# A decoder layer in one fp32 kernel: memory laid out from two ends, loads of the next phase begun early, x1 kept transposed, and GpSimd making sums and down's blocks

## The chip, the cores and the metric

The kernel runs on one core of one Trainium2 chip. It has five engines that each take their instructions in order: PE (TensorE, matrix products), DVE (VectorE), ACT (ScalarE), POOL (GpSimd) and SP (SyncE), which here issues every data transfer. An engine that has to wait stands, and everything behind the waiting instruction stands with it. The metric is the device time of one execution in microseconds (us); less is better.

## The reference

Inputs are x (1, 2048, 1024), a conditioning vector and the weights, all fp32. One layer has two sub-layers, each followed by a layer norm:

```python
for l in range(DEPTH):                                   # DEPTH = 1
    mod = (sc @ w_ada[l] + b_ada[l])[:, None, :]
    sh1, s1, g1, sh2, s2, g2 = jnp.split(mod, 6, axis=-1)
    u = x * (1 + s1) + sh1
    x = layer_norm(DN_ALPHA * x + g1 * token_mixer(u, ...), ln1_g[l], ln1_b[l])
    u = x * (1 + s2) + sh2
    x = layer_norm(DN_ALPHA * x + g2 * swiglu(u, w_gate[l], w_up[l], w_down[l]), ln2_g[l], ln2_b[l])

def swiglu(u, w_gate, w_up, w_down):                     # 1024 -> 2816 -> 1024
    return (jax.nn.silu(u @ w_gate) * (u @ w_up)) @ w_down
```

token_mixer holds two kinds of windowed attention, whose outputs are lifted to 1024 channels (w_a, w_b), merged by sigmoid gates and projected by w_o. The x after the first layer norm is called x1 below.

## The kernel before

Every product is made with fp32 accuracy from parts: ScalarE rounds an operand to its high part (hi, L114), VectorE subtracts this from the operand (lo, L115), and PE makes three passes, hi x hi, hi x lo and lo x hi. This pair of instructions is a split.

**Attention, to about 830 us**, is left as it is by the change. **The mixer's end, 830 to 1500 us**, goes over four chunks of 512 tokens in the order 3, 0, 1, 2. For each, PE makes the gates (L147, mm<-ut,whl), w_a and w_b, then the out-projection with w_o (L881, outputs in banks s and o). VectorE adds the residual and takes statistics (L887 to L890) and finishes the layer norm (layer_norm, L737 and L738, on tiles named xr), and SP stores x1 to DRAM (x_s). The next chunk's gates do not read this.

**The FFN, 1500 to 2430 us**, multiplies by w_gate and w_up with a Strassen-Winograd scheme of seven products. It runs in 44 sets: two passes p over halves of the tokens, 11 groups g of 256 of the 2816 columns, and gate and up in turn. A set is 84 matmuls of 128x512: seven products of 12, in the order 1, 6, 2, 7, 5, 4, 3. Set 0 of each pass and the last set of each pass run by block (k = 0 to 3, all seven products for each k), the others by product. A set needs left factors, made once per pass by left(p, k) from x1, and right factors, made for each set by the class Right:

- left loads four blocks of x1, PE transposes them (L945), ScalarE applies scale and shift (L946), VectorE makes four sums (left_sums, L907 to L910), and two splits give the tiles cb.
- Right loads 1 MB of weights (L959, tile g, "the raw block"), VectorE makes four sums (right_sums, L913 to L916, t1 to t4), and splits give the units a, b, c and d (tiles w). The raw block of set N+1 is asked for while set N runs.
- Of the results, ScalarE and VectorE form the four output quarters (L996, silu L1007, up times gate L1019). Product 3 adds into the bank that product 5 left, so VectorE has to have read the bank by then. After each up set GpSimd makes four left sums of h (L907 to L910), and h and the sums are stored in DRAM (h_s).

**The down phase, 2430 us to the end**, uses the same seven products over 77 steps of 24 matmuls (L1149, acc<-hw). For each step factors(m, g) loads 128x1024 of h_s and 128x512 of w_down or of its sums (t_s), and splits it (tile hw). right_of makes the sums of w_down on VectorE during the first 11 steps. first_half, second_half and evict multiply by g2 (g2b, on GpSimd at L1168 or VectorE), add the residual and make the last layer norm.

Each phase's buffers lie in pools that are opened when the phase begins and closed at its end; a pool's buffer is reused only when everything that reads it has ended. The order of the instructions on each engine is settled when the kernel is built, in the order of the code with a scheduler's shifts.

## Time and profile before

| | |
|---|---|
| median of 3 runs | 2906.16 us (2901.02 to 2907.05) |
| the profiled execution | 2909.35 us, its span 2907.5 us |
| mean granted clock of TensorE | 0.975 |
| TensorE busy | 2762.3 us, 95% |
| VectorE busy | 1959.4 us, 67% |
| ScalarE busy | 1161.7 us, 40% |
| GpSimd busy | 255.8 us, 9% |

The span runs from the first to the last instruction. The granted clock is the share of TensorE's full clock that the chip gave in that stretch, 1.00 being all of it. Busy time leaves out waits, so what an engine lacks to the span is time in which it stood. In the rows below, "out<-in" names the tiles that an instruction writes and reads.

### The profile page before, as it was taken

To read this page: it belongs to the slowest core of one execution; us is meant where nothing else is said; L and a number is where in the kernel's file an instruction comes from. 1 tells how busy PE (TensorE), PEld (TensorE's weight loads), DVE (VectorE), ACT (ScalarE), POOL (GpSimd) and SP (SyncE) were. 2 spreads that over 40 slices of the span, in tenths; PEclk is the share of its full clock that TensorE was granted. 3 is DMA by queue.
4 is the path that set the end of the run, shared out by engine and by line. 5 is a ranking of instruction groups with operands and counts; after the bars stand their busy time and mean duration, and the time that the engine had idled before them with its cause. 6 is when DMAs were issued, how large, how long until landed. Compare 5 with 4: busy or idle time off the path is not lost. (4 is left out here: it accounts for less than half of the span.)

```text
span 2907.5 us, 37081 instructions
## 1 busy us (share of the span) xinstructions
PE 2762.3 (95%) x13715; PEld 2292.2 (79%) x13715; DVE 1959.4 (67%) x3459; ACT 1161.7 (40%) x1918; POOL 255.8 (9%) x163
## 2 busy tenths in 40 slices
PE   7999999999999999999978999996999997999986
PEld 6888888887887788888866888885888886888875
DVE  7656567778768876756367666667666664543499
ACT  3555455666695443342324223234222222333220
POOL 0000000000000000000000111111111110000233
PEclk9999999999999999999989999997999998999998
DMA  9764646776788664744323223333233225984463
GB/s 281 198 157 127 164 117 145 165 176 141 158 204 287 198 207 144 219 127 150 110 95 98 94 94 98 109 123 98 95 109 109 94 95 209 329 279 143 144 218 125
DMA packets 569797, 452.98 MB, mean 156 GB/s; under 512 B 205640, under 2 KB 486288, under 8 KB 569616
## 3 DMA queue, kind: packets, MB, share of 16 engines
q1 hardware_dynamic: 569616, 450.62, 53.0%
q8 instruction: 107, 1.75, 0.3%
q14 instruction: 74, 0.61, 0.1%
HBM read 322.80 MB, written 91.82 MB: 143 GB/s over the span
## 5 line engine op out<-in xcount | busy, mean ns | idle before, releaser
L992 PE MATMUL mm<-cb,w 128*128 128x512 f32 x3696 | 860.2, 394 | 31.7 <-ACT w L114 12.3
L992 PEld LDWEIGHTS mm<-cb,w 128*128 128x128 f32 x3696 | 698.7, 190 | 184.9 <-ACT w L114 13.6
L147 PE MATMUL mm<-ut,whl 128*128 128x512 f32 x3072 | 727.7, 394 | 3.9 <-DVE ut L115 3.5
L147 PEld LDWEIGHTS mm<-ut,whl 128*128 128x128 f32 x3072 | 571.8, 188 | 131.3 <-DVE ut L115 7.0
L1149 PE MATMUL acc<-hw 128*128 128x512 f32 x1848 | 427.5, 394 | 36.8 <-ACT hw L114 18.7
L1149 PEld LDWEIGHTS acc<-hw 128*128 128x128 f32 x1848 | 351.4, 191 | 112.9 <-ACT hw L114 19.2
L115 DVE TENSOR_TENSOR whl<-raw,whl 128x1024 fp32r<-128x1024 f32 (+1 forms) x228 | 265.6, 1165 | 154.2 <-ACT whl L114 149.1
L114 ACT ACTIVATE whl<-raw 128x1024 fp32r<-128x1024 f32 (+1 forms) x228 | 230.3, 1010 | 308.6 <-PE mm L147 71.6
L114 ACT ACTIVATE w<-g 128x1024 fp32r<-128x1024 f32 (+1 forms) x176 | 167.0, 952 | 367.6 <-PE mm L992 329.1
L115 DVE TENSOR_TENSOR hw<-raw,hw 128x1536 fp32r<-128x1536 f32 x77 | 147.8, 1919 | 121.9 <-ACT hw L114 118.1
L114 ACT ACTIVATE hw<-raw 128x1536 fp32r<-128x1536 f32 x77 | 114.7, 1490 | 284.6 <-PE acc L1149 119.2
L115 DVE TENSOR_TENSOR w<-g,w 128x1024 fp32r<-128x1024 f32 (+1 forms) x176 | 194.4, 1108 | 37.5 <-ACT w L114 37.3
L560 PE MATMUL mm<-whl,ut 128*128 128x256 f32 (+1 forms) x1152 | 209.8, 340 | 0.0
L560 PEld LDWEIGHTS mm<-whl,ut 128*128 128x128 f32 x1152 | 202.7, 236 | 2.4
L996 DVE TENSOR_TENSOR t<-mm,t 128x512 f32<-128x512 f32 x138 | 94.9, 688 | 134.7 <-PE mm L992 134.7
L287 DVE TENSOR_TENSOR ehl<-te,ehl 128x512 f16<-128x512 f32 (+1 forms) x160 | 98.1, 615 | 109.9 <-ACT ehl L286 109.6
L147 PE MATMUL mm<-q,whl 128*128 128x512 f32 x576 | 138.2, 395 | 2.0 <-DVE q L115 1.2
L147 PEld LDWEIGHTS mm<-q,whl 128*128 128x128 f32 x576 | 109.9, 191 | 26.0 <-issue 1.5
L745 POOL TENSOR_TENSOR rs<-rs,mhalf 128x1 f32<-128x1 f32 x32 | 46.5, 1459 | 848.7 <-DVE rs L744 848.7
L907 POOL TENSOR_TENSOR g<-g 128x512 f32<-128x512 f32 x22 | 45.6, 2073 | 767.4 <-DVE g L1019 712.0
L276 DVE CUSTOM_DVE_ANT_0 te<-s,tab 128x256 f32<-128x256 f32 (+1 forms) x320 | 109.3, 382 | 1.7 <-PE s L264 1.4
L299 PE MATMUL o<-v,pt 128*128 128x192 bf16 x1096 | 92.3, 236 | 4.2 <-DMA pt<-ehl 4.2
(176 smaller groups left out, 2864.4 us busy)
## 6 DMA issues: line engine op xcount, KB each, us to landing
raw<-in_w_in_dram SPq DMA_DIRECT2D x132, 512.0 KB, 4.1
raw<-h_s SPq DMA_DIRECT2D x77, 512.0 KB, 3.7
g<-in_w_gate_dram SPq DMA_DIRECT2D x22, 1024.0 KB, 7.6
g<-in_w_up_dram SPq DMA_DIRECT2D x22, 1024.0 KB, 5.3
h_s<-g SPq DMA_DIRECT2D x22, 1024.0 KB, 5.1
h_s<-g SPq DMA_DIRECT2D x22, 768.0 KB, 3.5
raw<-in_w_ada_dram SPq DMA_DIRECT2D x32, 512.0 KB, 4.5
raw<-in_w_o_dram SPq DMA_DIRECT2D x32, 512.0 KB, 3.7
```

What stands on the lines that cost most here:

```text
L114: nc.scalar.activation(hi, src, AF.Copy)
L115: nc.vector.tensor_tensor(lo, src, hi.bitcast(F32), op=OP.subtract)
L147: nc.tensor.matmul(ps, lhs(k, a), rhs(k, b), start=i == 0, stop=i == n - 1)
L276: nc.vector.tensor_tensor_reduce(out=te[:, h, :nk], in0=ps[h], in1=tables[h][:, 256 - nk:], scale=1.0, scalar=-3e38, op0=OP.add, op1=OP.ma ...
L287: nc.vector.tensor_tensor(eh[:, 1], te[:, :, :nk], eh[:, 0], op=OP.subtract)
L299: nc.tensor.matmul(pv[:, h, a:], pt[:, (a * 2 + h) * nb + j], v[:, :3 - a], start=j == 0 and a == 0, stop=j == nb - 1 and a == 1)
L560: nc.tensor.matmul(ps[t][:, :n], lhs_of(us[k][a], t), whl[:, b, kk * n:(kk + 1) * n], start=k == 0 and i == 0, stop=k == KT - 1 and i == 2)
L745: nc.gpsimd.tensor_tensor(rs, rs, mhalf, op=OP.pow)
L907: eng.tensor_tensor(s[:, 0], a21, a22, op=OP.add)
L992: nc.tensor.matmul(ps, r.of(m, k, a), us[k][b][:, LEFT[m]], start=first and k == 0 and i == 0, stop=last and k == 3 and i == 2, skip_group ...
L996: nc.vector.tensor_tensor(out, ps, other, op=op)
L1149: nc.tensor.matmul(ps, hw[:, a, t * 128:(t + 1) * 128], hw[:, b, 1024:], start=first and i == 0, stop=last and i == 2, skip_group_check=True)
```

## The change

- Pools can be opened at either end of the memory (side="right"), so that buffers of the next phase are there while the current phase still holds its own. open_right opens the FFN's first buffers before the last out-projection of the mixer; open_down opens the down phase's before the last set of the FFN ends.
- x1 is also kept transposed in DRAM (xT_s). Chunks 3, 0 and 1 are transposed by PE at the chunk's end and copied by ScalarE; the 512 tokens of chunk 2 by turn, in sets 4 and 8 of the FFN. left_load then loads transposed blocks, without PE.
- GpSimd makes the left sums of the FFN's inputs (before: VectorE).
- down_right, after sets 2, 6, ..., 42: GpSimd scales w_down by g2 and makes its sums, eight blocks of a group go to t_s. The down phase reads them, and its multiplications by g2b are gone.
- All raw blocks, left blocks and down_right's two tiles share one pool of four buffers (g1). Before, six buffers g4 served these and h; now g4 has two, for h and its sums.
- The first half's layer norm in the down phase is done in two parts (first_left, first_right), its last part on ScalarE and GpSimd.

```diff
+    def g1():
+        return gp.tile([128, 4, 512], F32, name="g1")
...
+    def left_load(p, k):
+
+        e, s = g1(), g1()
+        nc.sync.dma_start(e[:, 1:3], dr(xT_s, (k + 4) * 128 * S + p * 1024, [[S, 128], [512, 2], [1, 512]]))
+        for hf in range(2):
+            nc.sync.dma_start(e[:, 3 * hf], dr(xT_s, k * 128 * S + p * 1024 + hf * 512, [[S, 128], [1, 512]]))
+        for kk, i in ((k, slice(0, 1)), (k, slice(3, 4)), (k + 4, slice(1, 3))):
+            nc.scalar.activation(e[:, i], e[:, i], AF.Identity, scale=mod[:, S2, kk:kk + 1],
+                                 bias=mod[:, SH2, kk:kk + 1])
+        left_sums(s, e[:, 0], e[:, 1], e[:, 3], e[:, 2], nc.gpsimd)
+        return e, s
+
+    def left_split(es, comb):
+
+        hi, lo = (comb.tile([128, 7, 512], F32R, name="cb") for _ in range(2))
+        split(hi[:, :3], lo[:, :3], es[0][:, :3])
+        split(hi[:, 3:], lo[:, 3:], es[1])
+        return hi, lo
+
+    def open_right():
+
+        nonlocal gp, comb, us01, es2, raw0, t0
+        gp = tile_pool(tc, "g1", 4, ctx, "right")
+        comb = tile_pool(tc, "comb1", 4, near, "right")
+        us01 = [left_split(left_load(0, k), comb) for k in range(2)]
+        raw0, t0 = load_right(w_gate, 0), g1()
+        gate_sums(t0, raw0)
+        es2 = left_load(0, 2)
...
+    def open_down():
+
+        nonlocal rawp, hwa, ready
+        rawp = tile_pool(tc, "raw5", 3, ctx, "right")
+        hwa = tile_pool(tc, "hwa", 3, ctx, "right")
+        ready = [factors(n) for n in range(AHEAD)]
...
+            if after is None:
+                outer.close()
+                open_right()
...
+            for k in range(KT if after is not None else 0):
+                ps = bank()
+                for b in range(4):
+                    nc.tensor.transpose(ps[:, b * 128:(b + 1) * 128], xr[b][:, k * 128:(k + 1) * 128], ident)
+                ub = ubp.tile([128, 512], F32, name="ub")
+                nc.scalar.activation(ub, ps, AF.Copy)
+                nc.sync.dma_start(xT_s[k, :, ch * 512:(ch + 1) * 512], ub)
...
+        g4 = pool("g4", 2, ph)
...
+        def down_right(g):
+
+            b, t = g1(), g1()
+            v = b.rearrange("p a n -> p (a n)").rearrange("p (f n) -> p f n", f=2)
+            nc.sync.dma_start(v, dr(w_down, 2 * g * 128 * D, [[D, 128], [128 * D, 2], [1, D]]))
+            for f in range(2):
+                nc.gpsimd.tensor_tensor(v[:, f], v[:, f], g2b, op=OP.mult)
+            right_sums(t[:, 0], t[:, 1], t[:, 2], t[:, 3], b[:, 0], b[:, 1], b[:, 2], b[:, 3], nc.gpsimd)
+            for i, x in enumerate((t, b)):
+                nc.sync.dma_start(dr(t_s, (g * 8 + i * 4) * 128 * 512, [[512, 128], [128 * 512, 4], [1, 512]]), x)
+
+        def turn(k0):
+
+            x, t = g1(), g1()
+            nc.sync.dma_start(x, dr(x1_s, 1024 * D + k0 * 128, [[D, 128], [128 * D, 4], [1, 512]]))
+            for k in range(4):
+                ps = mm_bank()
+                for b in range(4):
+                    nc.tensor.transpose(ps[:, b * 128:(b + 1) * 128], x[:, b, k * 128:(k + 1) * 128], ident)
+                nc.scalar.activation(t[:, k], ps, AF.Copy)
+            nc.sync.dma_start(dr(xT_s, k0 * 128 * S + 1024, [[S, 128], [128 * S, 4], [1, 512]]), t)
...
-            left_sums(s, e[:, 0], e[:, 1], e[:, 3], e[:, 2], nc.vector)
...
+        us = us01 + [left_split(es2, comb2), left_split(left_load(0, 3), comb2)]
         nxt = []
+
+        def between(k):
+            if k == 1:
+                near.close()
+                open_down()
...
+                             lambda k: nxt.append(left_split(left_load(1, k), comb if k < 2 else comb2)))
...
+            if n % 4 == 2:
+                down_right(n // 4)
+            if n in (4, 8):
+                turn(n - 4)
...
-            eng.tensor_tensor(y[:, hs], y[:, hs], g2b[:, hs], op=OP.mult)
...
-                w = xrp.tile([128, D], F32, name="xr")[:, :512]
-                nc.vector.tensor_tensor(w, ps, g2b[:, L], op=OP.mult)
-                nc.vector.tensor_tensor(x, x, w, op=OP.subtract)
-                nc.vector.bn_stats(sts[t][:, 0], x)
-                mv, rs = layer_norm(tmp, y, sts[t], l2g, l2b, t == 7)
+                nc.vector.tensor_tensor(x, x, ps, op=OP.subtract)
+                nc.vector.bn_stats(sts[t, 1][:, 0], x)
...
+        def first_left(t):
+            residual(y1[t], L, t, 0)
+            statistics(t, 0)
+            nc.vector.bn_stats(sts[t, 0][:, 0], y1[t][:, L])
+
+        def first_right(t):
             y = y1[t]
-            residual(y, slice(0, D), t, 0, nc.gpsimd)
-            st = tmp.tile([128, 2, 6], F32, name="st", bufs=9)
-            for n, hs in enumerate((L, R)):
-                nc.vector.bn_stats(st[:, n], y[:, hs])
-            layer_norm(tmp, y, st, l2g, l2b)
+            residual(y, R, t, 0)
+            nc.vector.bn_stats(sts[t, 0][:, 1], y[:, R])
+            mv, rs = layer_norm(tmp, y, sts[t, 0], l2g, l2b, True)
+            nm = tmp.tile([128, 1], F32, name="nm")
+            nc.vector.scalar_tensor_tensor(nm, mv[:, :1], -1.0, rs, op0=OP.mult, op1=OP.mult)
+            nc.scalar.activation(y, y, AF.Identity, scale=rs, bias=nm)
+            nc.gpsimd.tensor_tensor(y, y, l2g, op=OP.mult)
+            nc.gpsimd.tensor_tensor(y, y, l2b, op=OP.add)
             store(y, t, 0)
 
-        def second_half(t):
+        def second(t):
             x, z = y2[t][:, L], y2[t][:, R]
-            nc.vector.tensor_tensor(z, z, x, op=OP.add)
-            residual(y2[t], slice(0, D), t, 1, nc.gpsimd)
-            sts[t] = tmp.tile([128, 2, 6], F32, name="st", bufs=9)
-            nc.vector.bn_stats(sts[t][:, 1], z)
-
```

The change moves instructions at places that the prediction speaks of. On PE, at the end of chunk 0 (xr holds the rows of the layer norm, yl those of an attention output, ut and whl the next chunk's input and weights), the rows of before are these:

```order
L881 MATMUL s<-whl,mT 128x512 x12
L881 MATMUL o<-whl,mT 128x512 x12
L147 MATMUL mm<-ut,whl 128x512 x48
L147 MATMUL mm<-q,whl 128x512 x18
L199 MATMUL mm<-ones,adacc 128x1 x8
```

and these stand there now:

```order
L974 MATMUL s<-whl,mT 128x512 x12
L974 MATMUL o<-whl,mT 128x512 x12
L906 MATMUL s<-ident,yl 128x128 x8
L906 MATMUL o<-ident,yl 128x128 x8
L994 MATMUL mm<-ident,xr 128x128 x32
L149 MATMUL mm<-ut,whl 128x512 x48
L149 MATMUL mm<-q,whl 128x512 x18
```

The transposes of xr have come between the out-projection and the next chunk's gates, at the ends of chunks 3, 0 and 1; those of yl stood within the out-projection before.

On SP, in the first sets of the FFN, the transfers of before are, from the raw block of set 3 (up) to that of set 5:

```order
L959 DMA g_15627<-in_w_up_dram 128x8x256
L1107 DMA h_s<-g_15372 128x3x512
L1108 DMA h_s<-g_15620 128x4x512
L959 DMA g_15749<-in_w_gate_dram 128x8x256
L959 DMA g_15880<-in_w_up_dram 128x8x256
```

and now, where g_15861 and g_15862 are down_right's tiles b and t, and g_15872 the raw block of set 4:

```order
L783 DMA g_15739<-in_w_up_dram 128x8x256
L1023 DMA g_15861<-in_w_down_dram 128x2x1024
L1203 DMA h_s<-g_15484 128x3x512
L1204 DMA h_s<-g_15732 128x4x512
L1028 DMA t_s<-g_15862 128x4x512
L1028 DMA t_s<-g_15861 128x4x512
L783 DMA g_15872<-in_w_gate_dram 128x8x256
L783 DMA g_16003<-in_w_up_dram 128x8x256
```

The load of w_down and two stores have come ahead of the gate's raw block, which takes the buffer that t has left.

On DVE, the sums of that gate block (set 4) stood between the adds of set 2 and the splits of set 3 (g_15749 is the raw block, t_15632 a sum of set 2's products, w_15711 to w_15746 the units of set 3):

```order
L996 TENSOR_TENSOR t_15632<-mm,t_15631 128x512
L913 TENSOR_TENSOR g_15782<-g_15749 128x512
L996 TENSOR_TENSOR g_15629<-mm,t_15632 128x512
L914 TENSOR_TENSOR g_15782<-g_15749 128x512
L115 TENSOR_TENSOR w_15711<-g_15661,w_15711 128x1024
L915 TENSOR_TENSOR g_15782<-g_15749,g_15782 128x512
L996 TENSOR_TENSOR g_15629<-t_15632,mm 128x512
L916 TENSOR_TENSOR g_15782<-g_15782,g_15749 128x512
L115 TENSOR_TENSOR w_15729<-g_15661,w_15729 128x1024
```

and now begin set 3; from the second of them (t_15875 is the first sum of set 3's products, g_16003 the raw block of set 5, and t_15953 the sum that reads the bank of product 5):

```order
L771 TENSOR_TENSOR g_15905<-g_15872 128x512
L772 TENSOR_TENSOR g_15905<-g_15872,g_15905 128x512
L773 TENSOR_TENSOR g_15905<-g_15905,g_15872 128x512
L1081 TENSOR_TENSOR t_15875<-mm,t_15874 128x512
L770 TENSOR_TENSOR g_16037<-g_16003 128x512
L771 TENSOR_TENSOR g_16037<-g_16003 128x512
L772 TENSOR_TENSOR g_16037<-g_16003,g_16037 128x512
L773 TENSOR_TENSOR g_16037<-g_16037,g_16003 128x512
L1099 TENSOR_TENSOR g_15741<-mm,g_15741 128x512
L117 TENSOR_TENSOR w_15923<-g_15872,w_15923 128x1024
L1081 TENSOR_TENSOR t_15876<-mm,t_15875 128x512
L1081 TENSOR_TENSOR t_15953<-mm,t_15876 128x512
```

All eight sums have moved ahead of the second and third add of set 3, and the gate's four ahead of its first.

## Rows read from the trace of the kernel before

**Rows 1.** The page's busy times by engine, and its chain that ended last.

```profile
PE 2762.3 (95%) x13715; PEld 2292.2 (79%) x13715; DVE 1959.4 (67%) x3459; ACT 1161.7 (40%) x1918; POOL 255.8 (9%) x163
...
PE 10%; DVE 4%; POOL 1%; DMA 1%; issue 0%; SPq 0%; ACT 0%; DVEq 0%; ACTq 0%; POOLq 0%
```

**Rows 2.** Windows: stretch, length, busy by engine (instructions), granted clock, DMA share, GB/s.

```profile
1500.00:1563.00 63.00, 35.94 (x144) 25.16 (x145) 46.23 (x56) 28.97 (x29) 5.42 (x4) 0.77 0.37 117
...
1700.00:1900.00 200.00, 200.00 (x884) 165.65 (x883) 137.01 (x159) 58.06 (x74) 41.61 (x24) 1.00 0.33 107
1900.00:2000.00 100.00, 82.77 (x369) 64.92 (x367) 70.13 (x76) 41.98 (x47) 14.45 (x8) 0.90 0.33 102
2000.00:2100.00 100.00, 93.80 (x387) 76.39 (x388) 63.56 (x75) 27.47 (x35) 14.34 (x8) 0.93 0.34 111
...
2420.00:2480.00 60.00, 41.27 (x176) 33.51 (x175) 31.15 (x32) 14.00 (x10) 5.42 (x4) 0.86 0.77 279
...
2850.00:2907.50 57.50, 35.47 (x138) 27.65 (x137) 52.30 (x72) 1.48 (x1) 18.15 (x11) 0.81 0.25 95
```

**Rows 3.** Timeline of PE at the FFN's second pass: start, length, what, [idle before].

```profile
2001.96 20.05 PE L992 MATMUL mm<-cb,w 128*128 128x512 f32 x74 [8.03 <-ACT w L114]
2026.24 26.10 PE L992 MATMUL mm<-cb,w 128*128 128x512 f32 x102 [4.23 <-ACT w L114]
```

**Rows 4.** Timeline of PE at the end of chunk 0.

```profile
1161.37 2.96 PE L881 MATMUL o<-whl,mT 128*128 128x512 f32 x12
1164.17 11.05 PE L147 MATMUL mm<-ut,whl 128*128 128x512 f32 x48
```

**Rows 5.** Timeline of DVE behind it: a split, and the norm's last operations.

```profile
1171.71 1.22 DVE L115 TENSOR_TENSOR whl<-raw,whl 128x1024 fp32r<-128x1024 f32 x1
...
1177.84 2.48 DVE L738 SCALAR_TENSOR_TENSOR xr<-xr,rs,l1b 128x1024 f32<-128x1024 f32 x2
```

**Rows 6.** Timeline of PE at the start of the FFN.

```profile
1496.72 2.96 PE L881 MATMUL o<-whl,mT 128*128 128x512 f32 x12
1500.64 0.66 PE L945 MATMUL tr<-ident,g 128*128 128x128 f32 x4 [0.96 <-DVE xr L888]
...
1518.56 1.09 PE L945 MATMUL tr<-ident,g 128*128 128x128 f32 x4 [8.73 <-DMA g<-x_s]
...
1562.33 21.88 PE L992 MATMUL mm<-cb,w 128*128 128x512 f32 x91 [0.15 <-DVE cb L115]
```

**Rows 7.** ACT from 1500 us on, by line: busy, mean ns, idle before.

```profile
L1032 ACT ACTIVATE t<-mm 128x512 f32<-128x512 f32 x40 | 23.9, 597 | 49.5 <-PE mm L992 49.3
L114 ACT ACTIVATE cb<-g 128x2048 fp32r<-128x2048 f32 x8 | 15.3, 1909 | 27.2 <-DVE g L910 27.2
```

**Rows 8.** DMA issues from 1490 us on: count, KB each, median us to landing.

```profile
g<-in_w_up_dram SPq DMA_DIRECT2D x22, 1024.0 KB, 5.3
h_s<-g SPq DMA_DIRECT2D x22, 1024.0 KB, 5.1
g<-in_w_gate_dram SPq DMA_DIRECT2D x21, 1024.0 KB, 7.6
...
g<-x_s SPq DMA_DIRECT2D x28, 256.0 KB, 4.2
```

**Rows 9.** Timeline of POOL: the left sums of one h.

```profile
1698.60 2.16 POOL L907 TENSOR_TENSOR g<-g 128x512 f32<-128x512 f32 x1 [31.27 <-DVE g L1019]
...
1704.22 1.62 POOL L910 TENSOR_TENSOR g<-g,g 128x512 f32<-128x512 f32 x1
```

**Rows 10.** POOL by line: the multiplication by g2b.

```profile
L1168 POOL TENSOR_TENSOR y<-y,g2b 128x1024 f32<-128x1024 f32 x16 | 44.8, 2821 | 339.5 <-ACT hw L114 308.5 <-DVE y L1212 31.0
```

**Rows 11.** Timeline of DVE beside those left sums and after them.

```profile
1698.38 1.22 DVE L115 TENSOR_TENSOR w<-g,w 128x1024 fp32r<-128x1024 f32 x1
1699.77 0.69 DVE L996 TENSOR_TENSOR t<-mm,t 128x512 f32<-128x512 f32 x1 [0.17 <-PE mm L992]
...
1701.23 1.78 DVE L1019 TENSOR_TENSOR g<-t,g 128x512 f32<-128x512 f32 x1
...
1706.32 0.68 DVE L915 TENSOR_TENSOR g<-g,g 128x512 f32<-128x512 f32 x1
...
1714.22 0.69 DVE L913 TENSOR_TENSOR g<-g 128x512 f32<-128x512 f32 x1 [2.83 <-DMA g<-in_w_gate_dram]
```

**Rows 12.** Timeline of PE in the down phase: its first row and its last waits.

```profile
2448.84 26.46 PE L1149 MATMUL acc<-hw 128*128 128x512 f32 x109 [18.73 <-ACT hw L114]
...
2818.77 33.00 PE L1149 MATMUL acc<-hw 128*128 128x512 f32 x133 [9.14 <-DVE y L1189]
2856.58 1.65 PE L1149 MATMUL acc<-hw 128*128 128x512 f32 x3 [4.81 <-DVE hw L115]
2862.35 32.05 PE L1149 MATMUL acc<-hw 128*128 128x512 f32 x128 [4.12 <-DVE hw L115]
```

More of the change, by code (lines that the diff above doesn't have):

```diff
@@ L50, with tile_pool @@
 SCALE = HD ** -0.5
-def tile_pool(tc, name, bufs, stack):
-    return stack.enter_context(tc.tile_pool(name=name, bufs=bufs, reuse_waits="tile"))
+def tile_pool(tc, name, bufs, stack, side="left"):
+    return stack.enter_context(tc.tile_pool(name=name, bufs=bufs, side=side, reuse_waits="tile"))
 @with_exitstack
@@ L74, in trunk @@
     h_s = dram.tile([FT // 2, 7, 128, 1024], F32, name="h_s")
-    t_s = dram.tile([FT // 2, 4, 128, 512], F32, name="t_s")
+    t_s = dram.tile([FT // 2, 8, 128, 512], F32, name="t_s")
+    xT_s = dram.tile([KT, 128, S], F32, name="xT_s")
     ident = consts.tile([128, 128], F32, name="ident")
@@ L748, in layer_norm, with left_sums @@
         return mv, rs
+    A11, A12, A22, A_1, A_2, A_3, A_4 = range(7)
+    LEFT = {1: A11, 2: A12, 3: A_4, 4: A22, 5: A_1, 6: A_2, 7: A_3}
+    T3, T1, T2, T4, B11, B12, B21, B22 = range(8)
+    RIGHT = {1: B11, 2: B21, 3: B22, 4: T4, 5: T1, 6: T2, 7: T3}
+    G = FT // 2
+    AHEAD = 3
+    steps = [(m, g) for m in (1, 2, 6, 5, 3, 7, 4) for g in range(G)]
+    near = ctx.enter_context(ExitStack())
+    def left_sums(s, a11, a12, a21, a22, eng):
+        eng.tensor_tensor(s[:, 0], a21, a22, op=OP.add)
+        eng.tensor_tensor(s[:, 1], s[:, 0], a11, op=OP.subtract)
+        eng.tensor_tensor(s[:, 2], a11, a21, op=OP.subtract)
+        eng.tensor_tensor(s[:, 3], a12, s[:, 1], op=OP.subtract)
@@ new lines, in gate_sums @@
+    def gate_sums(t, raw):
+        r = by_k(raw)
+        t3, t1, t2, t4 = (t[:, i].rearrange("p (k c) -> p k c", k=4) for i in range(4))
+        right_sums(t3, t1, t2, t4, r[:, :4, :128], r[:, :4, 128:], r[:, 4:, :128], r[:, 4:, 128:], nc.vector)
+    def left_load(p, k):
[8 more added lines that the diff above has]
+        return e, s
@@ new lines, in trunk, with factors @@
+    gp = comb = us01 = es2 = raw0 = t0 = None
+    def factors(n):
+        m, g = steps[n]
+        raw = rawp.tile([128, 1536], F32, name="raw")
+        nc.sync.dma_start(raw[:, :1024], dr(h_s, (g * 7 + LEFT[m]) * 128 * 1024, [[1024, 128], [1, 1024]]))
+        nc.sync.dma_start(raw[:, 1024:], t_s[g, RIGHT[m]])
+        hw = (hwa if n % 7 < 3 else hwb).tile([128, 2, 1536], F32R, name="hw")
+        split(hw[:, 0], hw[:, 1], raw)
+        return hw
+    def open_down():
[3 more added lines that the diff above has]
+        ready = [factors(n) for n in range(AHEAD)]
@@ L966, in sums @@
                 self.b22 = r[:, 4:, 128:]
-                self.t = big()
-                t3, t1, t2, t4 = (self.t[:, i].rearrange("p (k c) -> p k c", k=4) for i in range(4))
-                right_sums(t3, t1, t2, t4, r[:, :4, :128], r[:, :4, 128:], r[:, 4:, :128], self.b22)
+                self.t = g1() if t is None else t
+                if t is None:
+                    gate_sums(self.t, self.raw)
             def unit(self, n):
@@ L1077, in trunk @@
         sets = [(p, g, w) for p in range(2) for g in range(G) for w in (w_gate, w_up)]
-        rights = {n: Right(sets[n][2], sets[n][1]) for n in range(1)}
-        rights[0].sums()
+        rights = {0: Right(sets[0][2], sets[0][1], raw0)}
+        rights[0].sums(t0)
         for n in "abcd":
             rights[0].unit(n)
-        us = [left(0, k) for k in range(4)]
+        us = us01 + [left_split(es2, comb2), left_split(left_load(0, 3), comb2)]
         nxt = []
+        def between(k):
+            if k == 1:
+                near.close()
+                open_down()
         for n, (p, g, w) in enumerate(sets):
@@ L1098, in trunk @@
             elif g == G - 1 and w is w_up:
-                set_by_block(us, r, sink, then, None if p else lambda k: nxt.append(left(1, k)))
+                set_by_block(us, r, sink, then, between if p else
+                             lambda k: nxt.append(left_split(left_load(1, k), comb if k < 2 else comb2)))
                 us = nxt
@@ L1236, in trunk @@
                 side.pop(0)()
-            if g == G - 1 and m == 3:
-                side = [partial(first_half, t) for t in range(8)]
-            if g == G - 1 and m == 7:
-                side = [partial(second_half, t) for t in range(8)]
+            if g == G - 1 and m in (2, 3, 7):
+                side += [partial({2: first_left, 3: first_right, 7: second}[m], t) for t in range(8)]
         for f in side:
```

135 lines of the change are left out of this document (48 added, 87 removed).

## The prediction

> **What bounds the kernel now.** I read the page first: TensorE is busy 95% of the span, VectorE 67%, GpSimd 9%, and the chain that ended last is a tenth PE and little else [rows 1]. So the time is the matmuls plus the places where PE stands. The windows show these places: full stretches with the clock at 1.00, and four holes. They lie where the FFN begins (1500 to 1563, PE 35.94 of 63), where its second pass begins (1900 to 2000, 82.77 of 100), where the down phase begins (2420 to 2480) and at the end [rows 2]. In a full stretch 884 matmuls take 200 us, 0.226 us each: a set of 84 is 19.0 us, a product of 12 is 2.7 us. In the holes the granted clock is below 1.00 too: after a wait of 8.03 us, 74 matmuls took 20.05 us where 74 x 0.226 is 16.7 [rows 3], so a long wait costs up to 3.3 us more than itself. Since PE is bound by its own order, I then asked of each moved row what stands ahead of it on its engine.
>
> The sum goes against the profiled execution, 2909.35 us (span 2907.5 and 1.9 around it); the median of the runs is 2906.16, 3.2 less. A change of less than 0.2% (6 us) can't be told from none.
>
> **Chunk ends, +58.** Before, the next chunk's matmuls follow the out-projection with no gap (1161.37 + 2.96, next at 1164.17) [rows 4]. Now 32 transposes of xr stand between, after chunks 3, 0 and 1, and they read the finished layer norm. VectorE ends that norm at 1180.3 [rows 5], 16 us after the last matmul; two weight splits of 1.2 us lie within it, so I take 15. Then come the transposes (four in 0.66 us [rows 6]) and their copies by ScalarE (0.6 us each [rows 7]), which have to free the bank of the next matmuls: 3.5 more. 18.5 x 3 = 55.5. The transposes of yl that move into the gap had cost about 3 in all. For the clock I add 2.5 per gap (0 to 3.3). Bounds: 35, if the splits and some of the norm are out of the way, to 65. Nothing covers this: PE is in order, and all work of the next chunk is behind it.
>
> **FFN start, -20.** Set 0 took from 1499.7 to about 1563.9 (80 of the window's 144 matmuls are products, so four are missing), 64 us instead of 19 [rows 2, 6]: transposes, a load of x1 that is waited for 8.73 us, splits. Now blocks k = 0 and 1 and the first gate factors are made inside the last out-projection, and no transposes are left. But VectorE has the layer norm of the last chunk to finish first (15 us), and block 3 can be loaded only when the splits of block 2 leave a buffer, about 16 us after the chunk. Its load of x takes about 5 (4.2 for a block of a quarter of it [rows 8]), ScalarE's four scalings 2.5, GpSimd 7.2 [rows 9], the split 4 (1.9 on ScalarE [rows 7], as much again on VectorE): about 36. Set 0 ends about 39 after the chunk, and set 1 starts some 5 late, since its sums are late next: 44 against 64. Bounds -30 to -12.
>
> **Down's blocks made in the FFN (down_right), +75.** This is the dearest term. In eleven gate sets (N = 2, 6, ..., 42) GpSimd scales two 128x1024 blocks and forms four sums behind the left sums of h, which end 6.2 us into the set (1705.84, the set before having ended at 1699.6) [rows 9, 11]. A 128x1024 mult took 2.82 us; four such sums took 7.2 [rows 9, 10]. 2 x 2.8 + 7.2 = 12.8, so GpSimd ends 19.0 into set N, as set N+1 begins. Behind it on SP's queue stand the two stores to t_s, and then the gate load for set N+2, which needs the buffer of the first store: 5.1 for a store of 1024 KB and 7.6 for the gate load [rows 8], and 0.8 for SP's issues. So this raw block lands about 13.5 into set N+1. In VectorE's new order its four sums stand ahead of set N+1's first add, and the four sums of the up block stand behind that add. After the landing VectorE needs eight sums, four operations on 128x512 at 0.69 and a split of 1.22 [rows 11] to reach the one that reads the bank of product 5: 9.5, thus 23 into the set. Product 3 adds into this bank and would begin at 16.3. PE waits 6.5 us. For N = 2 to 38 that is ten times: 65, and 1 us each for the clock. Before, the gate's raw block was late too, but only 2.83 us for VectorE, which stood ahead of no bank that PE needed [rows 11]. Bounds: 0, if the block lands 6.5 us sooner; 8.5 x 10 + 3.3 x 10 = 118, if the up load slows the gate load. The cover that is gone is buffers: four g1 tiles serve what had six g4 tiles of their own before.
>
> The Trainium skill's GPSIMD Engine Reference, section 3.1 (Elementwise — side-by-side cycle accounting), gives 4497 ns for an add of 128x2048 on this engine; by half and a quarter of it, an estimate, the six operations would take 9.0 us, the wait would be 2.7 us, and the term about +30 instead of +75. This trace's rows are slower, since VectorE works beside them, and the sum stays with the rows.
>
> **Second pass, -10.** Before, set 21 and set 22 lost about 41 us in 1970 to 2050: 23.4 of idle PE (17.2 up to 2000 and 6.2 after [rows 2]), some 12 for 16 groups of four transposes, 6 of slow clock (3.3 after the wait of 8.03, and 102 matmuls in 26.10 instead of 23.1 after that of 4.23 [rows 3]). Now two free g1 buffers serve four left blocks one after the other: load 5, ScalarE 2.5, GpSimd 7.2, split 4, with only the last steps overlapping. Blocks 2 and 3 each wait for the splits of the block before: they end about 30 and 39 into set 21, and unit a of set 22 stands behind all of them on VectorE, at 45 to 49. Set 22 would begin at 19, so 28 are lost, and 3 of clock. Bounds -16 to +5.
>
> **Start of the down phase, -15.** The wait of 18.73 us [rows 12] is for the first split factors; they are now made in set 43. 3 to 6 us stay, for the last h stored and read back. Bounds -18 to -8.
>
> **Down phase, -21.** The multiplications by g2b, VectorE's sums of w_down and the two-step first half are gone or spread out. Three waits, 9.14, 4.81 and 4.12 [rows 12], were due to VectorE being full (52.30 of the last 57.5 us [rows 2]); I take 15 of these 18. The last matmul ends at 2894.4, 13 us before the span's end; with one operation fewer per tile 7 stay. Bounds -27 to -10.
>
> Counted in other terms or at nothing: two turns of 16 transposes in sets 4 and 8 (under 3 us each, set off in the -10 of the second pass); the stores to xT_s and t_s and the pools at two ends, since the DMA share of the FFN's windows is 0.33 or less [rows 2] and no queue but SP's holds them.
>
> Sum: 58 - 20 + 75 - 10 - 15 - 21 = +67. 2909.35 + 67 - 3.2 = 2973; I say 2970.
>
> **The rivals.**
> A, faster. The late gate block doesn't reach PE. VectorE is busy only 137.01 of 200 us in the FFN [rows 2], which speaks for it; that the sums are placed first in their set speaks against. It decides at about 6.5 us: if GpSimd's operations take their shorter times, or if the load takes 5.3 like the up load [rows 8], the wait falls to about 2 us or none. The sum without the term is -8: 2898; with 10 to 20 us of it left, 2908 to 2918.
> B. The chunk ends cost nothing: the norm would have to end within some 2 us of the last matmul and not at 16 [rows 5], or the transposes to find their xr done. Price 58: 2973 - 58 = 2915. The order speaks against it, the trace does too.
> C. GpSimd slows VectorE. Beside the left sums, VectorE's operations with two inputs in SBUF took 1.78 instead of 0.68 us [rows 11]. With 12.8 more us of GpSimd in every fourth set, about seven such operations stretch by 1.1: 7.7 us. VectorE has 6.0 us free per set (19.0 - 13.0), so alone this would hardly show. Where it falls behind the late block it lengthens the wait by up to 4.5 us: 10 x 4.5 = 45 more, 3015. The Trainium skill's GPSIMD Engine Reference, section 1 (Specifications), states this contention for VectorE instructions with two SBUF inputs; by that rule, the trace agrees (1.78 against 0.68).
> D. The second pass and FFN start gain what their gaps promise (45 and 41 rather than 20 and 10): 2973 - 56 = 2917.
>
> **How the numbers follow.** My forecast 0.58 (2935 to 3000 by itself), A 0.18, B 0.04, C 0.13, D 0.07. Predicted 2970. For 8 in 10 the range goes down to A and up to C: 2893 to 3015, which leaves out B and the tails of A and C. Faster by over 6 us is most of A and the lower tails of B and D, 0.19; within 6 us the rest of A and a little of B and D, 0.09; slower 0.72.
>
> **What would show it.** Chunk ends: three PE waits of 12 to 18 us for VectorE's norm (or ScalarE's copies) near 995, 1180 and 1370. Down_right: about ten waits of 3 to 9 us for VectorE, one in each odd pair of the FFN, with VectorE waiting for the gate load before them. FFN start: the first full run of matmuls about 40 us after the last chunk. Down: no wait over 7 us at its start and few later. I am wrong if the FFN sets run without waits, or if the three gaps are under 8 us.

## The result, and the profile after

The changed kernel takes 2983.09 us (median of 4 runs, 2972.89 to 2985.79), the kernel before 2904.8 in the same series: a ratio of 1.0262 (95% interval 1.0245 to 1.028), 78 us slower. The profiled execution has a span of 2979.7 us at a mean clock of 0.973, 72.2 us more than before.

The busy times by engine and the chain that ended last, of the changed kernel (as [rows 1]):

```profile
PE 2799.7 (94%) x13715; PEld 2293.6 (77%) x13715; DVE 1868.1 (63%) x3367; ACT 1181.6 (40%) x1950; POOL 440.0 (15%) x269
...
PE 49%; DVE 10%; DMA 7%; POOL 7%; issue 3%; ACT 1%; SPq 0%; DVEq 0%; POOLq 0%; ACTq 0%
```

VectorE has 91 us less work and GpSimd 184 us more, and PE is busy 37 us longer with the same 13715 instructions. That second number is the one to stop at; it returns below. The timelines of PE in both kernels, cut at the same places of the program, give this (us):

| stretch | before | changed | difference | forecast |
|---|---|---|---|---|
| to the end of chunk 2's out-projection | 1499.7 | 1564.7 | +65.0 | +58 |
| from there to where set 1 runs | 64.2 | 43.0 | -21.2 | -20 |
| from there to PE's wait for the down phase | 866.2 | 908.4 | +42.2 | +65 |
| PE's wait for the down phase | 18.7 | 6.4 | -12.3 | -15 |
| down phase | 458.7 | 457.3 | -1.4 | -21 |

PE at the end of chunk 1 in the changed kernel (start, length, what, idle before; as [rows 4]):

```profile
1371.65 2.88 PE L974 MATMUL o<-whl,mT 128*128 128x512 f32 x12
1382.16 2.31 PE L994 MATMUL mm<-ident,xr 128*128 128x128 f32 x8 [7.63 <-DVE xr L740]
1388.35 5.34 PE L994 MATMUL mm<-ident,xr 128*128 128x128 f32 x24 [3.87 <-DVE xr L740]
1393.45 0.72 PE L149 MATMUL mm<-ut,whl 128*128 128x512 f32 x2
```

From 1374.5 to 1393.5 PE makes no product: 19 us, in which it waits twice for the norm of a block of rows and then transposes. The transposes of the first rows begin before the last norm has ended, but all eight groups need the fourth block of rows.

The start of set 7 on POOL, SP, DVE and PE, one fence for each engine's timeline: GpSimd's work for down_right, the stores and the gate load behind it, VectorE's wait for that load, and PE's wait (as [rows 9, 11]):

```profile
1716.61 4.77 POOL L1025 TENSOR_TENSOR g<-g,g2b 128x1024 f32<-128x1024 f32 x2
...
1726.21 2.27 POOL L773 TENSOR_TENSOR g<-g,g 128x512 f32<-128x512 f32 x1
```

```profile
1728.50 0.91 SPq L1028 DMA_DIRECT2D t_s<-g  x2
1733.20 0.37 SPq L783 DMA_DIRECT2D g<-in_w_gate_dram  x1
```

```profile
1730.52 0.69 DVE L1081 TENSOR_TENSOR g<-mm,t 128x512 f32<-128x512 f32 x1 [0.47 <-PE mm L1077]
...
1741.13 0.69 DVE L770 TENSOR_TENSOR g<-g 128x512 f32<-128x512 f32 x1 [9.19 <-DMA g<-in_w_gate_dram]
...
1748.53 1.48 DVE L1081 TENSOR_TENSOR t<-mm,t 128x512 f32<-128x512 f32 x2
```

```profile
1750.07 24.16 PE L1077 MATMUL mm<-cb,w 128*128 128x512 f32 x96 [2.83 <-DVE t L1081]
```

Set 6 ended just before 1730.5 (VectorE's first row). The chain is the one forecast: GpSimd to 1728.48, the first store until the gate load can go at 1733.20, its landing at 1741.1, then four and four sums, and PE released at 1750.07. But each link is a little shorter, and PE waits 2.83 us, not 6.5. There are nine such waits, 1.2 to 3.1 us long, 19.7 in all; the tenth place, set 23, stands behind the second pass's long wait and has none.

PE at the second pass, and in the down phase (as [rows 3, 12]):

```profile
2045.11 1.22 PE L1077 MATMUL mm<-cb,w 128*128 128x512 f32 x2 [4.90 <-ACT w L116]
2073.79 16.47 PE L1077 MATMUL mm<-cb,w 128*128 128x512 f32 x59 [27.46 <-DVE w L117]
...
2522.43 47.90 PE L1216 MATMUL acc<-hw 128*128 128x512 f32 x202 [6.36 <-DVE t L1081]
...
2902.33 2.90 PE L1216 MATMUL acc<-hw 128*128 128x512 f32 x6 [18.63 <-DVE y L1260]
```

The last row is new. What stands behind it is seen on VectorE and GpSimd some 25 us earlier (timelines of both):

```profile
2877.57 0.16 DVE L1281 SCALAR_TENSOR_TENSOR nm<-mv,rs 128x1 f32<-128x1 f32 x1 [7.48 <-POOL rs L747]
```

```profile
2865.48 6.81 POOL L1283 TENSOR_TENSOR y<-y,g 128x1024 f32<-128x1024 f32 x2
2872.25 4.77 POOL L1284 TENSOR_TENSOR y<-y,g 128x1024 f32<-128x1024 f32 x2
2877.00 0.54 POOL L747 TENSOR_TENSOR rs<-rs,mhalf 128x1 f32<-128x1 f32 x1
```

GpSimd takes the power (rs) of a tile's variance in half a microsecond, but only after 11.5 us of multiplications and additions for other tiles; VectorE waits 7.48 us for it, with the next factors' split behind. From there to PE's row a second link follows, on SP and ACT:

```profile
2885.36 0.33 SPq L1245 DMA_DIRECT2D out_dram<-y  x1
2885.74 0.42 SPq L826 DMA_DIRECT2D raw<-t_s  x1
```

```profile
2889.23 1.48 ACT L116 ACTIVATE hw<-raw 128x1536 fp32r<-128x1536 f32 x1 [8.85 <-DMA raw<-t_s]
```

The store of a finished tile goes when GpSimd's last addition ends (2885.33), the load of the next factors stands behind it on SP, and ScalarE waits 8.85 us for that load.

And the windows 1780 to 1800 of the kernel before, where no wait lies, and of the changed kernel:

```profile
1780.00:1800.00 20.00, 20.00 (x90) 16.54 (x90) 13.34 (x17) 6.72 (x9) 1.92 (x2) 1.00 0.57 184
```

```profile
1780.00:1800.00 20.00, 20.00 (x87) 16.14 (x86) 15.81 (x21) 4.42 (x5) 5.60 (x4) 1.00 0.41 135
```

Same clock, PE busy all the time, no wait: 90 matmuls before, 87 now. Taken from the starts of successive matmuls in both traces, they come every 226.7 ns before and every 232.7 ns now, as a mean over the FFN; in the mixer's gates 227.2 and 233.4. 3612 matmuls (43 sets) x 6.0 ns are 22 us that no wait shows.

So the FFN's +42.2 divides like this, each set's time less 84 spacings: the nine late blocks 26.6 (waits and slow clock), the second pass 35.6 where it was 43.5, the two turns 3.5, the spacing 22; the sum, 26.6 - 7.9 + 3.5 + 22 = 44, leaves 2 for small losses of before that are gone.

### The profile page after: what moved, and what is told of

Its sections match the earlier page's. It is cut to its first block, busy times and chain, and to the rows that moved or that the text cites. A ratio compares the mean times of both kernels' runs of the same rounds, so it can differ in the third digit from the quotient of the medians.

```text
span 2979.7 us, 37189 instructions
## 1 busy us (share of the span) xinstructions
PE 2799.7 (94%) x13715; PEld 2293.6 (77%) x13715; DVE 1868.1 (63%) x3367; ACT 1181.6 (40%) x1950; POOL 440.0 (15%) x269
## 4 chain that ended last, share of the span: by engine, by line
PE 49%; DVE 10%; DMA 7%; POOL 7%; issue 3%; ACT 1%; SPq 0%; DVEq 0%; POOLq 0%; ACTq 0%
PE mm L1077 16%; PE mm L149 16%; PE acc L1216 11%; DMA g<-in_w_gate_dram 2%; PE mm L974 1%; POOL g L1025 1%; DMA t_s<-g 1%; DMA g<-in_w_down_dram 1%; DVE t L1081 1%; PE s L974 1%; PE o L301 1%; DVE w L117 1%; PE o L974 1%; DMA g<-in_w_up_dram 1%; POOL g L773 1%
## 5 line engine op out<-in xcount | busy, mean ns | idle before, releaser
L1077 PE MATMUL mm<-cb,w 128*128 128x512 f32 x3696 | 878.3, 400 | 69.4 <-DVE w L117 29.7
L149 PE MATMUL mm<-ut,whl 128*128 128x512 f32 x3072 | 744.3, 399 | 2.9 <-DVE ut L117 2.7
L117 DVE TENSOR_TENSOR hw<-raw,hw 128x1536 fp32r<-128x1536 f32 x77 | 140.7, 1829 | 201.8 <-ACT hw L116 201.7
L747 POOL TENSOR_TENSOR rs<-rs,mhalf 128x1 f32<-128x1 f32 x32 | 39.8, 1250 | 1041.6 <-DVE rs L746 1041.6
L764 POOL TENSOR_TENSOR g<-g 128x512 f32<-128x512 f32 x30 | 57.0, 1899 | 747.2 <-DVE g L1104 589.6
L770 DVE TENSOR_TENSOR g<-g 128x512 f32<-128x512 f32 x44 | 32.8, 745 | 125.8 <-DMA g<-in_w_gate_dram 94.1
```

Of the source, the lines that this page charges most:

```text
L117: nc.vector.tensor_tensor(lo, src, hi.bitcast(F32), op=OP.subtract)
L149: nc.tensor.matmul(ps, lhs(k, a), rhs(k, b), start=i == 0, stop=i == n - 1)
L747: nc.gpsimd.tensor_tensor(rs, rs, mhalf, op=OP.pow)
L764: eng.tensor_tensor(s[:, 0], a21, a22, op=OP.add)
L1077: nc.tensor.matmul(ps, r.of(m, k, a), us[k][b][:, LEFT[m]], start=first and k == 0 and i == 0, stop=last and k == 3 and i == 2, skip_group ...
```

## The experiments

Two theories were to be told apart for each place: PE's own order against the engines behind it at the chunk ends; buffers and SP's queue against slowing of VectorE beside GpSimd in the FFN; and, for the spacing, the place of the operands against the traffic beside PE. Unless said otherwise each kernel is the changed one with one edit; times are medians, ratios are to the kernel before. The kernel before took 2904.8 us beside the changed kernel and 2901.2 to 2902.9 beside the runs below, so a gain against the changed kernel is uncertain by some 3 us.

**Transposes within the next chunk (e1).**

```diff
-            for k in range(KT if after is not None else 0):
...
+            turned = partial(turn_x, ch, xr) if after is not None else None
...
+                if turned and m in (1, 2):
+                    turned(range(4 * m - 4, 4 * m))
```

> The changed kernel with only this undone in place: the transposes of a chunk's xr no longer stand at the chunk's end, but behind the second and third of the next chunk's eight gate steps (16 and 16). Theory (PE stands in order behind the finished norm): the three gaps of about 20 us at 993, 1184 and 1374 close, the transposes still cost PE about 4.5 us a chunk; 40 to 48 us are won, 2983 becomes about 2938. Rival (VectorE and ScalarE are what a chunk's end waits for, whatever PE's order is): the wait comes back inside the next chunk, and less than 15 us are won, 2968 or more.

Measured: 2937.13 us, 1.0126 (1.0106 to 1.0145). 46 us are won. PE, from the end of chunk 3 on:

```profile
989.75 0.39 PE L986 MATMUL o<-whl,mT 128*128 128x512 f32 x1
989.97 11.38 PE L149 MATMUL mm<-ut,whl 128*128 128x512 f32 x48
...
1020.78 2.26 PE L914 MATMUL mm<-ident,xr 128*128 128x128 f32 x16
1022.80 11.45 PE L149 MATMUL mm<-ut,whl 128*128 128x512 f32 x48
```

No gap at the chunk's end, and 2.0 us for 16 transposes inside. PE's order was the cause, and the wait does not come back inside the next chunk.

**The transposes alone, in the kernel before (e6).**

```diff
+    xT_s = dram.tile([KT, 128, S], F32, name="xT_s")
...
                 nc.sync.dma_start(x1_s[T * 128:(T + 1) * 128, :], xr[b])
+            for k in range(KT if after is not None else 0):
+                ps = bank()
+                for b in range(4):
+                    nc.tensor.transpose(ps[:, b * 128:(b + 1) * 128], xr[b][:, k * 128:(k + 1) * 128], ident)
+                ub = ubp.tile([128, 512], F32, name="ub")
+                nc.scalar.activation(ub, ps, AF.Copy)
+                nc.sync.dma_start(xT_s[k, :, ch * 512:(ch + 1) * 512], ub)
```

> The kernel before with one part of the change alone: at the ends of chunks 3, 0 and 1 PE transposes xr, ScalarE copies and SP stores it, as in the change; nothing reads the transposed copy, so this is the cost alone. Theory: three gaps of about 19 us each and their slow clock, 55 to 62 us over the kernel before, about 2963. Rival (the gaps of the changed kernel come from the changed places of the buffers and not from the order on PE): less than 20 us, under 2925.

Measured: 2959.25 us, 1.02 (1.0183 to 1.0217), 57.9 over its kernel before (2901.34). The term of +58 stands by itself, without any of the new places of the buffers.

**The gate's raw block asked for first (e2).**

```diff
+        early_raw = {}
...
-                r1 = rights[n + 1] = Right(sets[n + 1][2], sets[n + 1][1])
+                r1 = rights[n + 1] = Right(sets[n + 1][2], sets[n + 1][1], early_raw.pop(n + 1, None))
...
             if n % 4 == 2:
+                if n + 2 < len(sets):
+                    early_raw[n + 2] = load_right(sets[n + 2][2], sets[n + 2][1])
                 down_right(n // 4)
```

> The changed kernel with one thing moved: the gate's raw block of set N+2 is asked for ahead of down_right's loads and buffers, so that the up block of set N+3 takes the buffer that t leaves. Buffer theory (a raw block that stands behind the store of t comes too late, and VectorE waits for it ahead of the bank of product 5): the wait is not gone but moved to the up block, which now lands 16 to 19 us into set N+1 since w_down itself is loaded later; ten waits of 3 to 8 us instead of nine of 2 to 3, 0 to 50 us slower than the changed kernel, 2983 to 3033. Contention theory (VectorE is slowed beside GpSimd, whose work is the same): no change within 6 us, 2977 to 2989.

Measured: 2996.58 us, 1.0331 (1.0315 to 1.0348), 13.5 slower than the changed kernel. The timeline of DVE in set 7:

```profile
1733.24 1.67 DVE L770 TENSOR_TENSOR g<-g 128x512 f32<-128x512 f32 x1
...
1746.06 0.69 DVE L770 TENSOR_TENSOR g<-g 128x512 f32<-128x512 f32 x1 [4.68 <-DMA g<-in_w_up_dram]
```

The gate's sums begin at once, and now the up block is the one that comes late. PE waits at the same nine places, 2.6 to 4.2 us each, and the sets behind late blocks lose 40.1 us where they lost 26.6. GpSimd's work is the same, so the loss follows the buffers. The first row also shows the slowing that rival C spoke of (1.67 where it is 0.69 without GpSimd); it is there, but it didn't decide.

**Half blocks, one buffer (e5).**

```diff
-        def down_right(g):
-
-            b, t = g1(), g1()
...
+        def down_right(g, half):
+
+            x = g1()
...
-            if n % 4 == 2:
-                down_right(n // 4)
+            if n % 2 == 0:
+                down_right(n // 4, n // 2 % 2)
```

> The changed kernel with down_right done in halves of the columns, one half after each of the 22 gate sets, so that a half's block and its sums fit into one g1 buffer instead of two; GpSimd does the same arithmetic in twice as many, half as long operations. Buffer theory: two raw blocks and one half always find their buffers, the waits of 2 to 3 us for VectorE's add in every fourth set go and with them their slow clock; 30 to 45 us won, 2938 to 2953. Contention theory (the same GpSimd work beside VectorE): the waits stay or are spread out over more sets, less than 12 us won.

Measured: 2959.95 us, 1.0203 (1.0187 to 1.0218). 23 us are won, less than expected. All waits for VectorE's add are gone from the first and the second pass; PE runs sets without a break (1768.23, 1092 matmuls in 254.46 us):

```profile
1768.23 254.46 PE L1081 MATMUL mm<-cb,w 128*128 128x512 f32 x1092
```

That is the 26.6 of the nine late blocks. The start of the second pass became 9 us longer (45.0 instead of 35.6). Its first left block is asked for 2 us before set 21 and not 13 (2001.03 and 2007.47); that the half of set 20 holds its buffer until then is likely, but no run shows it. Buffers were the cause of the late blocks: the arithmetic on GpSimd is the same, and PE's waits are gone. The size that I had expected to win came from my forecast, not from the trace.

**The first half's stores three steps later (e3).**

```diff
-            store(y, t, 0)
+            if t >= 3:
+                store(y1[t - 3], t - 3, 0)
...
+            if t < 3:
+                store(y1[t + 5], t + 5, 0)
```

> The changed kernel with the stores of the first half's rows issued three steps later than the operations of GpSimd that they wait for; the same work on every engine. Queue theory (SP stands at such a store, and the loads of the next factors stand behind it): the wait of 18.6 us near the down phase's end goes, with its slow clock 16 to 22 us are won, about 2963. Rival (GpSimd's sixteen multiplications slow VectorE and are themselves what is waited for): less than 6 us are won, 2977 or more.

Measured: 2981.25 us, 1.0269 (1.0251 to 1.0287): nothing won that is clear of noise. PE's wait is 13.79 us at 2905.63 instead of 18.63, with ScalarE and VectorE still waiting for GpSimd's power before it (7.49 us on VectorE). So SP's queue is a link in this chain, worth some 5 us of the wait, but not what decides; as the cause of 16 to 22 us the theory fell. The rows of POOL above gave the next one: the power of a tile stands behind the multiplications of the tiles before it.

**The first half's norm on VectorE (e9).**

```diff
-            mv, rs = layer_norm(tmp, y, sts[t, 0], l2g, l2b, True)
...
-            nc.scalar.activation(y, y, AF.Identity, scale=rs, bias=nm)
-            nc.gpsimd.tensor_tensor(y, y, l2g, op=OP.mult)
-            nc.gpsimd.tensor_tensor(y, y, l2b, op=OP.add)
+            layer_norm(tmp, y, sts[t, 0], l2g, l2b)
```

> The changed kernel with the first half's last norm finished by VectorE in two operations of 128x1024 (as before the change) instead of one on ScalarE and two on GpSimd. Theory (GpSimd's power of the next tile's variance stands behind its two multiplications of 2.4 to 4 us, VectorE and ScalarE wait in order for it, and the splits of the next factors stand behind them): the wait of 18.6 us before product 7's end goes, 15 to 22 us won, about 2964. Rival (the waits come from the loads, which stand behind other transfers on SP): less than 6 us won.

Measured: 2957.81 us, 1.0197 (1.0183 to 1.0211). 25 us are won, more than the wait itself, and 24.5 of them lie in the down phase by the profiles. The edit takes away what the power stood behind and what the stores waited for, so it shows that GpSimd's two operations per tile are the cause and not which of the two ways costs how much. PE passes that place in one run:

```profile
2859.77 84.97 PE L1216 MATMUL acc<-hw 128*128 128x512 f32 x371
```

**The second pass's left sums on VectorE (e4).**

```diff
-        left_sums(s, e[:, 0], e[:, 1], e[:, 3], e[:, 2], nc.gpsimd)
+        left_sums(s, e[:, 0], e[:, 1], e[:, 3], e[:, 2], eng or nc.gpsimd)
...
-                             lambda k: nxt.append(left_split(left_load(1, k), comb if k < 2 else comb2)))
+                             lambda k: nxt.append(left_split(left_load(1, k, nc.vector), comb if k < 2 else comb2)))
```

> The changed kernel with the left sums of the second pass on VectorE instead of GpSimd (the first pass as it is). Theory (four blocks go one after the other through two buffers, each with 6 to 7 us of GpSimd in the chain): each of the four becomes 3 to 4 us shorter, the loss of about 35 us at the start of set 22 falls to about 22, 10 to 14 us won, about 2971. Rival (the loads and ScalarE's scalings of a block, or VectorE itself, set the pace): less than 5 us won.

Measured: 2975.24 us, 1.0258 (1.0241 to 1.0275), 8 us under the changed kernel by the medians, with intervals that overlap: the time alone shows no gain. By the profile the start of the second pass takes 28.3 us instead of 35.6 (the long wait 22.86 instead of 27.46). GpSimd is a part of that chain. What remains is loads, scalings and splits through two buffers by the order of the code; no run takes them apart.

**96 bytes left free at the far end (e8).**

```diff
     outer = ctx.enter_context(ExitStack())
+    space = ctx.enter_context(tc.tile_pool(name="space", bufs=1, side="right")).tile([128, 24], F32, name="space")
+    nc.vector.memset(space, 0.0)
```

> The changed kernel with 96 bytes per partition left free at the far end of the memory, so that each buffer laid out from that end begins at a multiple of 128 bytes instead of 32 bytes above one of 64; nothing else moves. Theory (the place of PE's operands makes its matmuls slower): in undisturbed stretches of the FFN with the clock at 1.00 a matmul starts every 232.7 ns in the changed kernel and every 226.7 in the kernel before; with the shift it is 226.7 again, in the FFN (3696 matmuls) and the mixer's gates (3744), 30 to 45 us won, about 2943. Rival (GpSimd's or the transfers' traffic beside PE slows it): the spacing stays at 232 to 234, less than 8 us won.

Measured: 2963.49 us, 1.021 (1.0196 to 1.0224). 20 us are won, less than expected, but the spacing did all that was said (window 1780 to 1800):

```profile
1780.00:1800.00 20.00, 20.00 (x90) 16.56 (x89) 11.30 (x12) 6.87 (x10) 16.89 (x10) 1.00 0.49 182
```

90 matmuls again, beside 16.89 us of GpSimd; over the FFN 226.8 ns, in the gates 227.3. The rival falls. The rest was given back at once: the waits for VectorE's add went from 19.7 to 31.6 us, and the nine late blocks cost about 46 instead of 26.6. A faster PE reaches the bank sooner; the block lands when it did. The slow matmuls had hidden a part of down_right's price.

**Half blocks and the 96 bytes (e12).** Both edits above.

> The changed kernel with two edits: down_right in halves and the 96 bytes left free. Theory (the shift gives back 40 us or more of matmul time, and the changed kernel with the shift alone won only 20 since a faster PE waits longer for the late gate blocks and gets a slower clock behind each wait): without the late blocks the shift is worth 38 to 45 us, 2960 becomes about 2918. Rival (the shift is worth 20 us and no more): 2940.

Measured: 2925.52 us, 1.0076 (1.0054 to 1.0098). Without the late blocks the shift is worth 34.4 us: nearer to the theory than to the rival, a little below its range. The spacing accounts for nearly all of it: 22 us in the FFN, about 10 in the mixer's gates (1584 matmuls at 6.1 ns less) and 2 in the down phase.

**The kernel before, all operands 32 bytes on (e11).**

```diff
+    space = ctx.enter_context(tc.tile_pool(name="space", bufs=1)).tile([128, 8], F32, name="space")
+    nc.vector.memset(space, 0.0)
     early = ctx.enter_context(ExitStack())
```

> The kernel before with 32 bytes per partition taken ahead of its pools, so that all buffers, the moving and the stationary operands of a matmul alike, begin 32 bytes above a multiple of 64; nothing else moves. If it is the place of each operand by itself that slows PE, the spacing of the matmuls rises from 226.7 to about 233 ns in gates, FFN and down phase and the kernel takes 40 to 60 us more. If it is the place of the one relative to the other, it stays within 6 us.

Measured: 2902.57 us, 1.0003 (0.9994 to 1.0012). Nothing: 226.8 ns in the FFN as before. It isn't the place of each operand that counts, but the one against the other.

**Four edits together (e7)** (transposes within the chunk, halves, later stores, the second pass's sums on VectorE).

> The changed kernel with the four edits together: transposes within the next chunk, down_right in halves, the first half's stores later, the second pass's left sums on VectorE. If each wait is a cause of its own, the gains add up: 45 + 38 + 19 + 12 = 114, about 2869, 35 us below the kernel before. If the waits hide one another, or VectorE becomes the bound, less: 2900 or more.

Measured: 2899.79 us, 0.9993 (0.9984 to 1.0003). The gains as measured one by one, 46 + 23 + 2 + 8 = 79, give 2904: they add up, and none is lost by the others. The forecast of 2869 was missed because it added the gains as expected, not as measured.

**Five edits together (e10)** (the same without the later stores, with the 96 bytes and the norm on VectorE).

> The changed kernel with five edits together: transposes within the next chunk, down_right in halves, the second pass's left sums on VectorE, the 96 bytes left free, and the first half's norm on VectorE. If the gains add up, 2983 - 46 - 23 - 8 - 40 - 19 = about 2847, 54 us below the kernel before (1.9%). If the place of the operands is no cause, about 2885.

Measured: 2843.07 us, 0.98 (0.9787 to 0.9813): 58 us below the kernel before, 140 below the changed one. The five gains one by one, 46 + 23 + 8 + 20 + 25 = 122, are less than that, since the shift is worth more once no block is late. PE's longest wait behind the mixer is 22.31 us at the second pass; in the down phase it makes one run:

```profile
2408.12 420.83 PE L1228 MATMUL acc<-hw 128*128 128x512 f32 x1845 [6.33 <-DVE t L1093]
```

## Why the prediction was right, and where only its sum was

The forecast of 2970 against 2983 was right in sign and in the two largest losses, and near in size; but three terms were off, and that their errors cancel is luck.

- **Chunk ends, +58:** 57.9 measured alone. The working held: norm, then transposes, then the next products. Only what was to show it (three waits of 12 to 18 us) came out smaller: PE waits twice or more in each gap, never over 7.63 us, with transposes between. The other 7 us of the mixer's +65 are not in the forecast: its gates' matmuls at 233.4 instead of 227.2 ns (about 10 us), a wait behind open_right's splits (2.53 us at 1546.90), and some 5 back from the out-projection, whose 768 matmuls come every 227.2 instead of 233.2 ns.
- **FFN start, -20:** -21.2. Set 0 ended 37.3 after the chunk (39 said), set 1 ran 43.0 after it (44 said).
- **down_right, +75:** the mechanism is right, by e2's and e5's runs, the term was mis-sized: 26.6. GpSimd took 11.9 us (1716.61 to 1728.48) where I had added up 12.8, and the landing came 10.7 us into the set, not 13.5; the way from there took 8.9 where I had said 9.5. In such a chain only what exceeds the slack is paid: product 3 begins about 16.3 us into the set, so a landing up to 7 us into it would cost nothing, and the 2.8 of the landing with half a us each from the way and from PE's slower pace made 3.7 of 6.5 disappear. At the old spacing the term is about 46. By an estimate from the 128x2048 add in the Trainium skill's GPSIMD Engine Reference, section 3.1, GpSimd's six operations would take 9.0 us; the trace's 11.9 lie nearer to the rows. The term of about +30 that followed from that estimate came nearer to 26.6 than mine, but by another way: GpSimd's operations were only 0.9 us shorter than I said, and the rest of the 3.7 lies on the way to and from the landing, in the length of the sets and in GpSimd's earlier start.
- **Second pass, -10:** -7.9 in sets 21 to 23.
- **Start of the down phase, -15:** -12.3.
- **Down phase, -21:** -1.4. The three waits of [rows 12] are gone, as the step said; the tail is 11.3 instead of 13.1, where the step had 7; what failed in the step is "gone or spread out" for the first half's norm. I priced what left VectorE and not what it met on GpSimd: a multiplication and an addition of 2.4 to 4 us per tile stand ahead of the next tile's power, for which VectorE and ScalarE wait with the splits of the next factors, and ahead of the stores that hold SP's queue. That is 18.63 us and the clock behind it (0.5 from 2887.89 to 2911.78); e9 gives 25 back.
- **What no step had:** +22 us in the FFN and about 10 in the mixer's gates from slower matmuls. "The pools at two ends" stood among the parts at nothing. I had asked what a pool's place does to the order and never what it does to PE's operands.

Of the rivals, B (no loss at the chunk ends) is refuted by e1 and e6. A (the late block doesn't reach PE) is refuted as a mechanism by e2 and e5, but its price is nearer than mine: the waits fell to 2.2 us on average, and 26.6 us were left where A allowed 10 to 20 and I had 75. C's slowing is visible in rows and didn't decide: in set 7 VectorE's sums behind the late block took 0.69 us each, with GpSimd done. D did not come: the FFN's start and the second pass gave 21 and 8. The sum came out because down_right was 48 too dear while the down phase (20), the spacing in the FFN (22) and the mixer's other 7 together cost 49 more than I had.

## What to carry to other kernels

A step that is put on an in-order engine costs whatever it waits for, however short it is: ask of each moved instruction what stands behind it, on GpSimd as well as on PE. Waits in a chain with slack are differences of two large numbers, so bound them by the shortest and the longest rows rather than by means, and expect them to grow when something else is made faster. When buffers move, compare the spacing of matmuls in a stretch without waits: 90 against 87 in 20 us is seen in no wait and no clock.

## What the runs showed of the hardware that was not expected

In this kernel an fp32 matmul of 128x512 comes every 227 ns or every 233 ns, at a granted clock of 1.00 in both, according to how far apart its two operands lie in a partition's memory. The moving operand is the one with 512 columns (cb, ut, hw, and whl in the out-projection), the stationary one that with 128 (w, whl, hw, and mT in the out-projection). The places are by the addresses in the built programs, in bytes above a multiple of 512, and the distance is moving less stationary, again above a multiple of 512; the times are means of the starts of successive matmuls.

| kernel and products | moving, stationary | distance | ns |
|---|---|---|---|
| before: FFN, gates, down phase | 128, 128 | 0 | 226.8, 227.3, 226.7 |
| before: out-projection | 128, 448 | 192 | 233.3 |
| before, 32 bytes on: FFN, gates, down phase | 160, 160 | 0 | 226.9, 227.3, 226.7 |
| before, 32 bytes on: out-projection | 160, 480 | 192 | 233.3 |
| changed: gates | 480, 128 | 352 | 233.3 |
| changed: FFN, cb of the first two blocks | 480, 128 | 352 | 234.1 |
| changed: FFN, cb of the last two blocks | 128, 128 | 0 | 231.4 |
| changed: out-projection | 128, 128 | 0 | 226.7 to 227.7 |
| changed: down phase | 128, 128 and 480, 480 | 0 | 227.4, 227.8 |
| 96 bytes free: FFN's first two blocks, gates | 384, 128 | 256 | 227.0, 227.4 |

Distances of 0 and 256 bytes give 227 ns, those of 192 and 352 give 233 to 234, in every kind of product. One row stands between, and the trace shows that the slowness outlasts the slow matmuls a little. Set 21 of the changed kernel runs by block; its 42 matmuls of the first two blocks come every 233.3 ns, the next eight, of the last two blocks, every 231.5, and the 33 after them every 226.7, in the same set, with GpSimd busy for 4.6 us of the last part's 6 (2033 to 2039). In a set by product the blocks change after six matmuls, so the last two never come down to 227. So the traffic beside PE is set aside by this trace too. Which other distances are bad was not measured, and why the distance counts stays open.
